# Expert stages with a reordered head and with the branch for over 192 rows at the stage's end

## The chip, the cores and the metric

The kernel runs on one core of a Trainium2 chip. The metric is the device time of one execution in microseconds (us); the time before is 1676.75 us, the median of three runs (1673.84 to 1679.83).

Engines in the profile: PE is TensorE (PEld its weight loads), DVE is VectorE, ACT is ScalarE, POOL is GpSimd, SP is SyncE, which mostly issues DMAs. A name with a q (DVEq) is the engine's queue: register loads, branches, semaphore and DMA-issuing instructions, which don't count as busy.

## The reference

A decoder trunk of two layers over 512 tokens of 1024 features, in fp32. Layer 0 mixes tokens with RWKV-7 and layer 1 with forgetting attention; each is followed by the same kind of expert layer (16 experts, the two best of one group of four for each token), and every sublayer ends in a residual sum and a layer norm:

```python
def shared_router_moe(h, router_w, router_bias, w_gate, w_up, w_down):
    s = jax.nn.sigmoid((xt @ router_w).astype(jnp.float32))
    s_sel = (s + router_bias).reshape(n_tok, N_GROUPS, EXPERTS_PER_GROUP)
    g_star = jnp.argmax(jnp.sum(lax.top_k(s_sel, 2)[0], -1), -1)
    ...
    gate = gate / jnp.sum(gate, -1, keepdims=True)
    ...
    def expert_block(args):
        xb, e = args
        hid = jax.nn.silu(xb @ w_gate[e]) * (xb @ w_up[e])
        return hid @ w_down[e]
    ...
def reference(...):
    for i in range(DEPTH):
        ...
        h = layer_norm(ALPHA * h + mixed, ...)
        ffn = shared_router_moe(h, ...)
        h = layer_norm(ALPHA * h + ffn, ...)
```

The lines left out pick the two best experts (`e_idx`) of the group, and sum each row of `expert_block`'s result, times its gate, into its token; `mixed` is the layer's token mixer, and DEPTH is 2. Each expert has a gate and an up matrix of 1024 x 512 and a down matrix of 512 x 1024. How many tokens an expert gets is known only when the kernel runs.

## The kernel before, in words

The order of stages is RWKV (about 0 to 519 us of the profiled execution), the experts of layer 0 (to 905), attention (to 1250), the experts of layer 1 (to 1640), and the last sum and layer norm. The program is scheduled by hand: on each engine instructions run in the order in which the code issues them.

Products keep fp32 accuracy by splitting each operand into a high part and a remainder (fp32r): ScalarE copies the high part (L199 for weights), VectorE subtracts (L202), and three matmuls add up one product (L68 to L70). Weights come in pieces of 1 MB, six for an expert: a ring of eight raw buffers and six pairs of split buffers. `wsplitA(m)` is the high copy of piece m, `wsplitB(m)` (also called `loA`) the subtraction, which then issues the load of piece m+8 on SP.

An expert stage is `moe` (L178). Its head:

- six high copies on ScalarE (L204), and the routing on VectorE (L207 to L229);
- `rows(n)` finds with one-hot matmuls which tokens the first two experts get, `gather` (L250) fetches 128 rows of the activations `hd` with an indirect DMA on POOL, and `gather2` (L257) the rows 129 to 192 of an expert as pairs of half rows into `xo`;
- `cnt`, the number of rows of each expert, `most`, the largest of them, and the subtraction of piece 0 (L262 to L267);
- `xposeT`/`xposeS` (L274) transpose and split the first expert's rows into Xm; `xposeB` (L303) does it with `xo`, into Xh; then the late loads (pieces 6 and 7, in layer 0 only, issued on ScalarE's queue) and `loA(1)`;
- the tables: VectorE computes for each slot the token, the target row and the gate (L394 to L417); eight scatters on POOL write them to `tab` in DRAM (L426), two loads bring them back as TB and TB2 (L430, L432);
- the If on `most>192` (L435), with `rest` for rows over 192 of an expert inside it. The data of this case never has so many, so every engine jumps over the body, and yet all go through it: they load `most` into a register, branch, and add to their semaphores. The body is 48 copies of `rest`, and it reloads the first six pieces (`again`) and pieces 6 and 7, and transposes the first rows again;
- `count(0)`, `count(1)` load an expert's row count into a register of all five engines; then `loA(2)` to `loA(5)`.

Then the loop over 16 experts: `count(e+2)`, `more(e)` (L338, an If on more than 128 rows: `guB`, `hidBT`, `dnB`, `outB` on the rows 129 to 192), the gathers for later experts, and `expert(e)` (L351): `guA` is gate and up, `dnA` is down, `outA` copies a half of the result, `scatter` (L333) writes the rows to `yd`. Between these an expert splits the next expert's weights and transposes its rows. `outB` (L331) writes its rows into `ys[0]` (`yt` in the profile) for the first expert; `gates0` (L418) makes the first expert's gate by matmul, so that it needs no table.

Behind the stage, `Combine.load_y` (L474) loads `yd` on SP (L478), ScalarE scales the residual (L481), PE adds (L486), and in layer 0 also spreads the norm's weights (L468, L471); VectorE does the layer norm.

Of the kernel before, what the change touches and what calls it, by code (L numbers as in the profile page):

```python
# [13 lines left out]
NR,NH,NM=8,6,6*NE  # L14
# [47 lines left out]
def split(C, hi, lo, src):  # L62
    nc=C.nc
    nc.scalar.activation(hi,src,AF.Copy)  # L64
    nc.vector.tensor_tensor(lo,src,hi.bitcast(F32),op=ALU.subtract)  # L65
# [107 lines left out]
def place(raw, L, W, m, queue):  # L173
    e,j=divmod(m,6); w,hf,kk,n=MAT[j]; M=W[w][L,ORDER[e]]
    queue.dma_start(raw.rearrange("p (k n) -> p k n",k=kk),(M[:,hf*n:(hf+1)*n] if w==1 else M[hf*128*kk:(hf+1)*128*kk,:]).rearrange("(k p) n -> p k n",p=128))


def moe(C, L, W, hd, load, tail, late=()):  # L178
# [4 lines left out]
    with ExitStack() as ctx:  # L183
# [13 lines left out]
        def wsplitA(m,q=None):  # L197
            if m<NM+tail:
                Q=slice(None) if q is None else QS[q]; nc.scalar.activation(his[m%NH][:,Q],raws[m%NR][:,Q],AF.Copy)  # L199
        def wsplitB(m,q=None):  # L200
            if m<NM+tail:
                Q=slice(None) if q is None else QS[q]; V.tensor_tensor(los[m%NH][:,Q],raws[m%NR][:,Q],his[m%NH][:,Q].bitcast(F32),op=ALU.subtract)  # L202
                if q!=0: load(m+NR)
        for m in range(NH): wsplitA(m)  # L204
        loA=wsplitB
        ss=su[:,0:64].rearrange("p (a b) -> p a b",b=4)
# [37 lines left out]
        def rows(n, e, oh, slots):  # L244

            for i in range(NT): V.tensor_scalar(oh[:,i,:],slots,posm[:,i,e:e+1],None,op0=ALU.is_equal)
            for i in range(NT):
                for c in range(2): nc.tensor.matmul(px[:,n:n+1],oh[:,i,:],C.aux[:,i,c:c+1],start=(i+c==0),stop=(i+c==NT))
            V.tensor_scalar(i01[:,n:n+1],px[:,n:n+1],8192.0,None,op0=ALU.add)
        def gather(ix,xg,n):  # L250
            nc.gpsimd.indirect_dma_start(out=xg[0:n],out_offset=None,in_=hd[:,:],  # L251
                in_offset=bass.IndirectOffsetOnAxis(ap=ix[0:n],axis=0),bounds_check=T-1,oob_is_err=False)
        for e in range(2): rows(e,e,oh[e],C.slots); gather(i01[:,e:e+1],xgs[e],128)

        oh2=ys[1][:,256:512].bitcast(BF16).rearrange("p (t n) -> p t n",t=NT); rows(2,0,oh2,C.slots2); i2=p1.tile([128,1],I32,name="i2")
        V.tensor_scalar(i2,i01[:,2:3],2.0,C.odd,op0=ALU.mult,op1=ALU.add)
        def gather2(e):  # L257

            nc.gpsimd.indirect_dma_start(out=xo,out_offset=None,in_=hd.rearrange("t (h n) -> (t h) n",h=2),  # L259
                in_offset=bass.IndirectOffsetOnAxis(ap=TB2[:,4*e+1,3:4] if e else i2,axis=0),bounds_check=2*T-1,oob_is_err=False)  # L260
        gather2(0)
        cnt=p1.tile([1,NE],I32,name="cnt"); V.tensor_copy(cnt,pp[0:1,NT,:])  # L262
        rs={}
        def count(e):
            if e<NE: rs[e]=nc.values_load(cnt[0:1,ORDER[e]:ORDER[e]+1],min_val=0,max_val=T,skip_runtime_bounds_check_because="a count of 512 tokens")
        most=p1.tile([1,1],I32,name="most"); V.tensor_reduce(most,cnt,axis=AX.X,op=ALU.max)
        loA(0); V.tensor_copy(sel,selb)  # L267

# [3 lines left out]
        def slot(m): return his[m%NH],los[m%NH]  # L272
        src=lambda e,b=0: TB[:,4*e+b,0:1]; dst=lambda e,b=0: TB[:,4*e+b,1:2]; gate=lambda e,b=0: TB[:,4*e+b,2:3].bitcast(F32); gate2=lambda e,b=0: TB2[:,4*e+b,2:3].bitcast(F32)
        def xposeT(xg,hf,bk):  # L274
            for k in range(4): nc.tensor.transpose(k4(bk)[:,k,:],xg[:,(hf*4+k)*128:(hf*4+k+1)*128],C.ident)  # L275
        def xposeS(hf,bk): split(C,Xm[:,0,hf*4:hf*4+4,:],Xm[:,1,hf*4:hf*4+4,:],k4(bk))
# [26 lines left out]
        def xposeB():  # L303
            pt=tr[0].rearrange("p (k t h) -> p h k t",k=4,h=2)
            for k in range(4): nc.tensor.transpose(k4(tr[0])[:,k,:],xo[:,k*128:(k+1)*128],C.ident)
            X=Xh.rearrange("p (h k) t c -> p h k t c",h=2)
            for h in range(2): split(C,X[:,h,:,:,0],X[:,h,:,:,1],pt[:,h])
# [43 lines left out]
        def expert(e):  # L351
            f,fo=(gate(e),None) if e else (None,g0[:,0:1]); y=ys[e%2]; w=[slot(6*e+j) for j in range(6)]
            X=xgs[(e+1)%2]; next_=e+1<NE
            hi=lambda j,*q: wsplitA(6*e+6+j,*q); lo=lambda j,*q: wsplitB(6*e+6+j,*q)
            guA(w[0],0); hi(0); lo(0)
            guA(w[1],1); siluA(); hi(1)
            if e==0: gates0(0)
            guA(w[2],2); mulA(0,f); hi(2); lo(1)
            guA(w[3],3,range(6)); hidT(0); hidS(0)
            guA(w[3],3,range(6,8)); mulA(1,f)  # L360
            if next_: xposeT(X,0,tr[1]); xposeS(0,tr[1])
            hi(3,0); lo(2,0)
            dnA(w[4],4,0); hidT(1); hidS(1); hi(3,1); lo(2,1)
            dnA(w[4],4,1)
            if next_: xposeT(X,1,tr[1]); xposeS(1,tr[1])
            hi(4); lo(3)
            dnA(w[5],5,0); outA(0,y,fo)
            if next_: xposeB()
            lo(4); dnA(w[5],5,1); outA(1,y,fo); scatter(dst(e),y,128); hi(5); lo(5)
        def again(e,j):  # L370
            r=raws[6+j%2]; w=slot(6*e+j); place(r,L,W,6*e+j,nc.gpsimd); split(C,*w,r); return w
        def rest(e,blk):

            f=gate(e,blk); ix=dst(e,blk)
            if blk==1: V.memset(i2[0:64],int(BIG)); V.tensor_copy(i2[64:128],ix[64:128]); ix=i2
            gather(src(e,blk),ys[0],128)
            for hf in range(2): xposeT(ys[0],hf,tr[hf]); xposeS(hf,tr[hf])
            for j in range(6):
                w=again(e,j)
                if j<4: guA(w,j)  # L380
                if j==1: siluA()
                if j in (2,3): mulA(j-2,f); hidT(j-2); hidS(j-2)
                if j>3:
                    for n in range(2): dnA(w,j,n)
            for n in range(2): outA(n,ys[0])
            scatter(ix,ys[0],128)

        for hf in range(2): xposeT(xgs[0],hf,tr[hf]); xposeS(hf,tr[hf])
        xposeB()
        for m in late: load(m,nc.scalar)  # L390
        loA(1)

        bl=su[:,256:320].rearrange("p (a b) -> p a b",b=NE); code=su[:,320:384].rearrange("p (a b) -> p a b",b=NE); pos=pp[:,0:NT,:]
        V.tensor_scalar(bl,pos,127.5,None,op0=ALU.is_gt)  # L394
# [36 lines left out]
        t2=tab[0:4096,:]  # L431
        nc.gpsimd.dma_start(TB2,bass.AP(tensor=t2.tensor,offset=t2.offset,ap=[[256,64],[0,2],[1,256]]))  # L432
        nc.gpsimd.tensor_scalar(TB2[:,:,3],TB2[:,:,0],2.0,C.odd,op0=ALU.mult,op1=ALU.add)

        with tc.If(nc.values_load(most[0:1,0:1],min_val=0,max_val=T,skip_runtime_bounds_check_because="a count of 512 tokens")>192):  # L435
            for e in range(NE):
                count(e)
                for blk in (1,2,3):
                    with tc.If(rs[e]>max(192,128*blk)): rest(e,blk)
            for j in range(NH): again(0,j)  # L440
            for m in (6,7): load(m,nc.gpsimd)
            for hf in range(2): xposeT(xgs[0],hf,tr[hf]); xposeS(hf,tr[hf])
        for e in range(2): count(e)
        for m in range(2,NH): loA(m)
        for e in range(NE):
            count(e+2)
            more(e)
            if e+2<NE or e==0: gather(src(2) if e==0 else src(e+2),xgs[e%2],128)
            if e+1<NE: gather2(e+1)
            expert(e)  # L450
    return yd

class Combine:
# [937 lines left out]
```

## Time and profile before

| | |
|---|---|
| median of three runs | 1676.75 us (1673.84 to 1679.83) |
| profiled execution | 1676.42 us, span 1674.7 us |
| granted TensorE clock, mean | 0.923 |
| PE busy | 1486.3 us, 89% of the span |
| VectorE busy | 1172.9 us, 70% |
| ScalarE busy | 926.9 us, 55% |
| POOL busy | 517.1 us, 31% |
| DMA | 317.77 MB, mean 190 GB/s |

Times of instructions count from the start of the span; 1.7 us of the profiled execution lie outside it. [...] A steady expert keeps PE almost fully busy, the stretches between two stages and a stage's head do not.

### The profile page before, as it was taken

What the parts mean: (1) busy time and instruction counts of PE and PEld (TensorE: products, weight loads), DVE (VectorE), ACT (ScalarE), POOL (GpSimd) and SP (SyncE); (2) the same over time, 40 slices, a digit from 0 to 9 for tenths busy, and PEclk for the clock granted to TensorE, in tenths of its full rate; (3) what the DMA queues carried; (4) which work ended last, traced back from release to release, by engine and by line L of the source; (5) the groups of instructions that cost most, each with busy time, mean ns of one, the idle gap of its engine ahead of it and who ended that gap; (6) DMA issues with size and microseconds to landing.
All of it is one profiled execution on the core that took longest, in us unless ns stands there. A gap on an engine that the chain in (4) does not pass through costs nothing. (4 is left out here: it accounts for less than half of the span.)

```text
span 1674.7 us, 25018 instructions
## 1 busy us (share of the span) xinstructions
PE 1486.3 (89%) x9185; PEld 1202.8 (72%) x9185; DVE 1172.9 (70%) x1883; ACT 926.9 (55%) x1361; POOL 517.1 (31%) x423
## 2 busy tenths in 40 slices
PE   6998976989984799999999799999973999999995
PEld 2587765977763688888886677777763788888883
DVE  7547769576785497877996637556545696869984
ACT  2543764534334386867885446555333686858863
POOL 4104776313331333322431422111013232413421
PEclk8998997788986899999999899999985999999998
DMA  7326532033515598897994323112433697979963
GB/s 216 120 82 217 155 97 69 13 121 95 172 68 178 185 340 297 300 350 251 353 353 169 102 82 113 63 36 75 151 107 134 227 370 237 362 243 353 350 235 152
DMA packets 203605, 317.77 MB, mean 190 GB/s; under 512 B 27978, under 2 KB 123554, under 8 KB 203444
## 3 DMA queue, kind: packets, MB, share of 16 engines
q1 hardware_dynamic: 181060, 276.13, 48.4%
q0 software_dynamic: 17664, 33.11, 5.8%
q10 hardware_dynamic: 4720, 6.44, 1.1%
q8 instruction: 93, 1.52, 0.4%
q14 instruction: 68, 0.56, 0.1%
HBM read 304.80 MB, written 37.55 MB: 204 GB/s over the span
## 5 line engine op out<-in xcount | busy, mean ns | idle before, releaser
L202 DVE TENSOR_TENSOR wl<-raw,wh 128x2048 fp32r<-128x2048 f32 (+1 forms) x168 | 334.5, 2005 | 16.9 <-DMA tab<-rec,idx 6.5
L199 ACT ACTIVATE wh<-raw 128x2048 fp32r<-128x2048 f32 (+1 forms) x168 | 282.6, 1688 | 13.3 <-ACT wh L199 8.7
L68 PE MATMUL bank<-wh,xm 128*128 128x256 f32 (+1 forms) x768 | 250.2, 326 | 3.9
L69 PE MATMUL bank<-wl,xm 128*128 128x256 f32 (+1 forms) x768 | 245.4, 320 | 0.0
L70 PE MATMUL bank<-wh,xm 128*128 128x256 f32 (+1 forms) x768 | 245.2, 319 | 0.0
L334 POOL DMA_INDIRECT yd<-yt,TB x38 | 91.5, 2407 | 447.8 <-ACT yt L301 387.5
L68 PEld LDWEIGHTS bank<-wh,xm 128*128 128x128 f32 x768 | 144.7, 188 | 26.1 <-issue 14.6
L69 PEld LDWEIGHTS bank<-wl,xm 128*128 128x128 f32 x768 | 144.8, 189 | 11.4
L70 PEld LDWEIGHTS bank<-wh,xm 128*128 128x128 f32 x768 | 144.7, 188 | 11.3
L202 DVE TENSOR_TENSOR wl<-rawo,wh 128x2048 fp32r<-128x2048 f32 (+1 forms) x56 | 110.2, 1980 | 20.6 <-ACT wh L199 20.1
L68 PE MATMUL bank<-wh,wh 128*128 128x512 f32 x256 | 112.7, 440 | 3.1 <-DVE wl L1082 1.7
L68 PE MATMUL bank<-wh,hm 128*128 128x512 f32 x256 | 111.3, 435 | 2.9 <-ACT hm L64 2.9
L70 PE MATMUL bank<-wh,wl 128*128 128x512 f32 x256 | 102.1, 399 | 2.8 <-DVE wl L1268 2.8
L69 PE MATMUL bank<-wl,wh 128*128 128x512 f32 x256 | 101.5, 397 | 0.0
L70 PE MATMUL bank<-wh,hm 128*128 128x512 f32 x256 | 101.4, 396 | 0.0
L69 PE MATMUL bank<-wl,hm 128*128 128x512 f32 x256 | 100.9, 394 | 0.0
L199 ACT ACTIVATE wh<-rawo 128x2048 fp32r<-128x2048 f32 (+1 forms) x56 | 93.4, 1668 | 12.8 <-PE bank L70 9.0
L1090 POOL TENSOR_TENSOR wl<-raw,wh 128x512 fp32r<-128x512 f32 x29 | 40.8, 1418 | 87.7 <-ACT wh L1089 87.7
L259 POOL DMA_INDIRECT xo<-hd,TB x30 | 61.9, 2063 | 13.0 <-issue 8.0
L65 DVE TENSOR_TENSOR xm<-bank,xm 128x512 fp32r<-128x512 f32 x64 | 44.3, 692 | 29.8 <-ACT xm L64 26.9
L64 ACT ACTIVATE xm<-bank 128x512 fp32r<-128x512 f32 x64 | 38.3, 598 | 47.7 <-PE bank L275 38.8
L68 PEld LDWEIGHTS bank<-wh,wh 128*128 128x128 f32 x256 | 49.6, 194 | 16.4 <-issue 5.6
(545 smaller groups left out, 3557.7 us busy)
## 6 DMA issues: line engine op xcount, KB each, us to landing
raw<-in_moe_w_gate_dram SPq DMA_DIRECT2D x48, 1024.0 KB, 8.4
raw<-in_moe_w_up_dram SPq DMA_DIRECT2D x48, 1024.0 KB, 9.9
raw<-in_moe_w_down_dram SPq DMA_DIRECT2D x48, 1024.0 KB, 7.1
rawo<-in_moe_w_up_dram SPq DMA_DIRECT2D x16, 1024.0 KB, 5.6
rawo<-in_moe_w_down_dram SPq DMA_DIRECT2D x16, 1024.0 KB, 7.8
rawo<-in_moe_w_gate_dram SPq DMA_DIRECT2D x14, 1024.0 KB, 8.9
raw<-in_fx_w_in_dram SPq DMA_DIRECT2D x12, 1024.0 KB, 6.6
raw<-in_rw_wk_dram SPq DMA_DIRECT2D x4, 1024.0 KB, 12.4
```

The lines of the kernel that those rows point to most:

```text
L64: nc.scalar.activation(hi,src,AF.Copy)
L65: nc.vector.tensor_tensor(lo,src,hi.bitcast(F32),op=ALU.subtract)
L68: nc.tensor.matmul(out,ah,bh,start=start,stop=False)
L69: nc.tensor.matmul(out,ah,bl,start=False,stop=False)
L70: nc.tensor.matmul(out,al,bh,start=False,stop=stop)
L199: Q=slice(None) if q is None else QS[q]; nc.scalar.activation(his[m%NH][:,Q],raws[m%NR][:,Q],AF.Copy)
L202: Q=slice(None) if q is None else QS[q]; V.tensor_tensor(los[m%NH][:,Q],raws[m%NR][:,Q],his[m%NH][:,Q].bitcast(F32),op=ALU.subtract)
L259: nc.gpsimd.indirect_dma_start(out=xo,out_offset=None,in_=hd.rearrange("t (h n) -> (t h) n",h=2), in_offset=bass.IndirectOffsetOnAxis(ap=T ...
L334: st=nc.gpsimd.indirect_dma_start(out=yd[:,:],out_offset=bass.IndirectOffsetOnAxis(ap=ix[0:n],axis=0), in_=y[0:n],in_offset=None,bounds_ch ...
L1090: (V if d else G).tensor_tensor(lo[n][:,Q],raw[:,Q],hi[n][:,Q].bitcast(F32),op=ALU.subtract)
```

## The change

The diff, cut to its changed lines:

```diff
@@ -201,6 +201,7 @@
                 if q!=0: load(m+NR)
+        for m in late: load(m,nc.scalar)
         for m in range(NH): wsplitA(m)
@@ -250,7 +251,8 @@
-        for e in range(2): rows(e,e,oh[e],C.slots); gather(i01[:,e:e+1],xgs[e],128)
+        def first(e): rows(e,e,oh[e],C.slots); gather(i01[:,e:e+1],xgs[e],128)
+        first(0)
 
...
@@ -259,10 +261,12 @@
         gather2(0)
+        first(1)
         cnt=p1.tile([1,NE],I32,name="cnt"); V.tensor_copy(cnt,pp[0:1,NT,:])
...
+        for e in range(2): count(e)
         most=p1.tile([1,1],I32,name="most"); V.tensor_reduce(most,cnt,axis=AX.X,op=ALU.max)
         loA(0); V.tensor_copy(sel,selb)
@@ -367,8 +371,6 @@
-        def again(e,j):
-            r=raws[6+j%2]; w=slot(6*e+j); place(r,L,W,6*e+j,nc.gpsimd); split(C,*w,r); return w
         def rest(e,blk):
@@ -376,7 +378,7 @@
             for j in range(6):
-                w=again(e,j)
+                r=raws[6+j%2]; w=his[2+j%4],los[2+j%4]; place(r,L,W,6*e+j,nc.sync); split(C,*w,r)
@@ -385,10 +387,6 @@
-        for hf in range(2): xposeT(xgs[0],hf,tr[hf]); xposeS(hf,tr[hf])
-        xposeB()
-        for m in late: load(m,nc.scalar)
-        loA(1)
 
...
@@ -431,16 +429,8 @@
         nc.gpsimd.tensor_scalar(TB2[:,:,3],TB2[:,:,0],2.0,C.odd,op0=ALU.mult,op1=ALU.add)
-
-        with tc.If(nc.values_load(most[0:1,0:1],min_val=0,max_val=T,skip_runtime_bounds_check_because="a count of 512 tokens")>192):
-            for e in range(NE):
-                count(e)
-                for blk in (1,2,3):
-                    with tc.If(rs[e]>max(192,128*blk)): rest(e,blk)
-            for j in range(NH): again(0,j)
-            for m in (6,7): load(m,nc.gpsimd)
-            for hf in range(2): xposeT(xgs[0],hf,tr[hf]); xposeS(hf,tr[hf])
-        for e in range(2): count(e)
+        for hf in range(2): xposeT(xgs[0],hf,tr[hf]); xposeS(hf,tr[hf])
+        loA(1); xposeB()
         for m in range(2,NH): loA(m)
         for e in range(NE):
             count(e+2)
@@ -448,6 +438,12 @@
             expert(e)
+
+        with tc.If(nc.values_load(most[0:1,0:1],min_val=0,max_val=T,skip_runtime_bounds_check_because="a count of 512 tokens")>192):
+            for e in range(NE):
+                count(e)
+                for blk in (1,2,3):
+                    with tc.If(rs[e]>max(192,128*blk)): rest(e,blk)
     return yd
```

In words: the late loads of layer 0 are issued before the six high copies; the gather of the first expert's half rows comes before that of the second expert's rows; the first two counts are loaded before piece 0 is subtracted; the table arithmetic and its scatters come before the first transposes, and `loA(1)` before `xposeB`. The If with `rest` stands behind the last expert, where the six split pieces of the first expert are no longer needed, so nothing is reloaded or transposed again in it; its weight loads are on SP's queue instead of POOL's.

## Rows read from the trace of the kernel before

**Rows 1.** Busy us (instructions) by stretch: stretch, length, engines, granted clock, DMA share, GB/s

```profile
520.00:552.00 32.00, 6.86 (x52) 4.96 (x53) 18.38 (x74) 13.67 (x11) 11.35 (x12) 0.50 0.69 240
...
593.00:612.00 19.00, 18.85 (x113) 16.28 (x113) 17.14 (x16) 15.46 (x16) 6.81 (x3) 1.00 0.98 332
```

**Rows 2.** Timeline, layer 0's head: start, us, engine, line, operation, out<-in, xcount [idle <-releaser]

```profile
528.88 2.29 DVE L202 TENSOR_TENSOR wl<-raw,wh 128x2048 fp32r<-128x2048 f32 x1
...
533.29 1.49 DVE L65 TENSOR_TENSOR xm<-bank,xm 128x512 fp32r<-128x512 f32 x2 [2.02 <-ACT xm L64]
...
537.22 1.09 PE L305 MATMUL bank<-ident,xo 128*128 128x128 f32 x4 [3.80 <-DMA xo<-hd,i]
...
539.23 0.95 ACTq L175 DMA_DIRECT2D rawo<-in_moe_w_gate_dram  x2
539.65 0.43 DVE L65 TENSOR_TENSOR xh<-bank,xh 128x256 fp32r<-128x256 f32 x1 [0.46 <-ACT xh L64]
540.00 2.28 DVE L202 TENSOR_TENSOR wl<-raw,wh 128x2048 fp32r<-128x2048 f32 x1
542.19 0.22 DVE L394 TENSOR_SCALAR su<-bank 128x64 f32<-128x64 f32 x1
...
547.15 0.40 DVE L416 CAST gp<-gr 128x4 bf16<-128x4 f32 x1
```

**Rows 3.** Timeline, layer 0, where the pair phase and the next subtractions begin

```profile
551.60 0.80 PE L309 MATMUL bank<-wl,xh 128*128 128x512 f32 x1 [3.74 <-DVEq L435]
...
554.02 8.90 DVE L202 TENSOR_TENSOR wl<-raw,wh 128x2048 fp32r<-128x2048 f32 x4 [6.47 <-DMA tab<-rec,idx]
```

**Rows 4.** Line L435, both layers: ns min/median/max, first and last start us, forms

```profile
L435 PEldq COMPARE_BRANCH  x2: 3718/3842/3967, 538.6 to 1275.2; - x2
...
L435 ACTq COMPARE_BRANCH  x2: 45/45/45, 541.3 to 1276.9; - x2
...
L435 POOLq TENSOR_LOAD <-most x2: 321/416/512, 571.2 to 1306.7; - x2
...
L435 POOLq INC_SWDGE_SEM  x2: 583/873/1163, 574.9 to 1310.2; - x2
```

**Rows 5.** Line L265 on ScalarE's queue, the heads of layers 0 and 1

```profile
L265 ACTq TENSOR_LOAD <-cnt x3: 278/280/291, 547.1 to 547.8; - x3
...
L265 ACTq TENSOR_LOAD <-cnt x3: 277/279/323, 1279.7 to 1280.4; - x3
```

**Rows 6.** Timeline, layer 0: expert 0's first matmul, the sum of outB, expert 1's first

```profile
569.48 0.40 PE L68 MATMUL bank<-wh,xm 128*128 128x512 f32 x1
...
576.17 0.68 DVE L331 TENSOR_TENSOR yt<-xo,bank 64x512 f32<-64x512 f32 x1 [9.68 <-DMA TB<-tab]
...
592.52 0.47 PE L68 MATMUL bank<-wh,xm 128*128 128x512 f32 x1
```

**Rows 7.** Timeline, layer 1: first transposes, pair phase, first matmuls of experts 0 and 1

```profile
1271.46 1.94 PE L275 MATMUL bank<-ident,xg 128*128 128x128 f32 x8 [9.91 <-DMA xg<-hd,i]
...
1288.07 0.79 PE L309 MATMUL bank<-wl,xh 128*128 128x512 f32 x1 [6.54 <-DVEq L435]
...
1304.63 0.39 PE L68 MATMUL bank<-wh,xm 128*128 128x512 f32 x1
...
1327.26 0.47 PE L68 MATMUL bank<-wh,xm 128*128 128x512 f32 x1
```

**Rows 8.** Timeline at the two stage ends: last scatter, loads of yd, scaling, adds

```profile
905.63 1.00 POOL L334 DMA_INDIRECT yd<-yt,TB  x1 [14.03 <-ACT yt L301]
...
908.33 0.34 SPq L478 DMA_DIRECT2D rawo<-yd  x1
...
1639.97 3.88 ACT L481 ACTIVATE raw<-raw 128x1024 f32<-128x1024 f32 x4
...
1641.07 7.13 PE L486 MATMUL bank<-raw,ident 128*128 128x512 f32 x16 [1.63 <-ACT raw L481]
...
1643.06 0.33 SPq L478 DMA_DIRECT2D rawo<-yd  x1
```

## The prediction

> **What bounds the kernel now.** I read the page's busy line first, then the busy shares by stretch, then the timeline around the branch at L435, then what that line's instructions do on each engine. The shares by stretch show two regimes [rows 1]. In a steady expert PE has work for 18.85 of 19.00 us: TensorE is the bound there, and nothing that the other engines save changes the time. In the head of a stage PE is busy for 6.86 of 32.00 us at half the clock: there the serial order of routing, gathers, tables and the first transposes sets the end, and each microsecond taken out of that chain moves all sixteen experts forward. So the change is priced in four places: two heads and two stage ends.
>
> In the head of layer 0 VectorE does the first expert's subtraction, then stands still for the gather, does xposeS, stands still again until the gather of the odd half rows lands (PE's transposes at L305 had waited 3.80 us for it), does the two halves of xposeB, then loA(1), and only then the table arithmetic [rows 2]. Then it walks through the If at L435. PE's phase of 64-row pairs (L309, guB in more(0)) starts one matmul, then waits for DVEq L435, that is for VectorE's passage through a branch whose body is not executed; the second matmul is at 551.60, and loA(2) to loA(5) begin at 554.02 behind it [rows 3]. The reader should see there that the releaser is a queue instruction, not data.
>
> The passage itself is dear [rows 4]: PE's compare-and-branch takes 3.7 to 4.0 us; ScalarE's takes 45 ns, but the engine's next instruction, the first count load, comes 5.8 us after it in layer 0 (541.3 to 547.1) and 2.8 us in layer 1 (1276.9 to 1279.7) [rows 4, 5]; POOL needs 3.7 and 3.5 us from its load of `most` to its INC_SWDGE_SEM, and that takes up to 1.2 more. POOL comes to this If last, behind the tables' landing, and holds the next thing up: VectorE's sum into yt (L331) waits 9.68 us, until 576.17, and expert 0 takes 23.04 us from its first guA matmul to that of expert 1, against 19.00 [rows 1, 6].
>
> **The change, part by part.**
>
> Head of layer 0. Removed from the path: the If, and the standstill before xposeB, because the table arithmetic now fills it. New order on VectorE: the counts, loA(0), sel, tables, xposeS, loA(1), xposeB. Before, loA(0) ran from 528.88 to 531.17 and sel closely behind it. The two counts come ahead of it now: a register load from SBUF takes 0.3 to 0.5 us on POOL and the three on ScalarE start over 0.7 us [rows 4, 5]; two of them with the wait on cnt I take as 1.0 (0.6 to 1.6). With 0.1 for sel, VectorE is free at 532.3, and the tables, 542.19 to 547.55 or 5.36 us, end at 537.65. xposeS 1.49 brings 539.15, loA(1) 2.28 brings 541.45, two xposeB subtractions of 0.43 with ScalarE's second copy between them (0.46) bring 542.8 [rows 2]. PE's phase then runs from about 542.9 instead of 551.60 less the half matmul that it had done early, 551.2 [rows 3]. Gain 8.3. loA(2) to (5) start then too, at the distance from guB that they have now.
>
> What is late next would be the gather. The two late loads, 2.1 MB, now share the DMA engines with the gathers instead of coming after them; at the stretch's mean of 240 GB/s [rows 1] that is 8.7 us of traffic. If all of it stood in front of the gather of xo, which lands at 537.2 now, the transposes would start at 545.9 and guB 2.9 us later (537.22 to 540.08, the end of xposeB, now), at 548.8: gain 2.4. If it costs nothing and the counts are at their lower end, 9.0. I take 8.3, because xposeS of the first gather now comes 4 us later than before, and xo is now second instead of third on POOL's queue. The two issues of the late loads (0.95 for both [rows 2]) go in front of ScalarE's six hi copies and delay each by as much; loA(0), which reads the first, starts a microsecond later too, so this is hidden. The gather of expert 1 moves behind xo; its rows are needed in the middle of expert 0. Tables, scatters and TB loads start 10 us earlier on POOL and DVE; nothing waits for them any longer in expert 0. The counts on PE, ScalarE, POOL and SP lie in front of the waits for the gather, hidden by those; SP has load(8) behind them, which waits for loA(0) anyway.
>
> Expert 0 of layer 0. With no If on POOL ahead, the sum into yt waits only for ScalarE's copy; ScalarE's hi(0) then follows and the weight splits run as in a steady expert. 19.0 and a margin of 0.4, which I chose, for its twelve small gate matmuls is 19.4 against 23.04: gain 3.6 (0 to 4.0).
>
> Layer 1 has no late loads. Its first gather is itself late: PE's transposes start at 1271.46 after 9.91 us of waiting for it [rows 7]. The tables (5.36) and the counts (1.0) fit into that wait. 1.94 for the transposes, with ScalarE's copy under them, 1.49, 2.28 and 1.32 (0.43, 0.46, 0.43) [rows 2] bring guB to 1278.5, against 1288.07, less half a matmul, 1287.7: gain 9.1 (7 if the counts delay a gather's issue by two, 12 if POOL's issue comes three earlier). Expert 0: 1327.26 less 1304.63 is 22.63, less 19.4: gain 3.2 (0 to 3.6).
>
> The four gains sum to 24.2; low ends 9.4, high ends 28.6. Later experts pass them on, since PE bounds these.
>
> Stage ends. The If now stands between expert 15 and what follows. End of layer 0: the last scatter is issued at 905.63 and takes 1.00; SP's first load of yd follows at 908.33, when it has landed [rows 8]. Behind the scatter POOL now loads `most`, branches, is silent and runs INC_SWDGE_SEM: 3.5 to 3.7 and 0.6 to 1.2, so 4.1 to 4.9 [rows 4], to 910.7 or 911.5. Everything that reads yd waits on that, as yt did in the head: 2.4 to 3.2, I take 2.8. ScalarE's passage, 0.4 and 2.8 [rows 4, 5], runs beside it; where it takes 5.8 the end costs 6.2. PE's 4.0 and its load, 4.4, lie beside ScalarE's passage, behind which the copies and the scaled rows come; only what exceeds that shows.
> End of layer 1: the same 2.8 for SP's load at 1643.06. ScalarE's scaling (1639.97) comes 3.2 later, PE's adds with it, at 1644.3, after an idle stretch of 4.8 instead of 1.63. The sixteen take 7.13 us now [rows 8]; in the heads' idle stretches the granted clock is 0.50 [rows 1], and all sixteen at that would cost 7.1 more. I take about a microsecond of it: 4.0 (2.4 to 10). Both ends: 6.8. [...]
>
> [...]
>
> Sum: the profiled execution took 1676.42 us (span 1674.7), 0.33 below the median of 1676.75. 1676.42 - 24.2 + 6.8 = 1659.0.
>
> **The rivals.**
> A, the forecast: 1659, own range 1653 to 1664.
> B, expert 0 keeps its length (the sum into yt is freed, but splits or scatters wait on another thing). For: the row of yt names the landing of TB<-tab as its releaser [rows 6]. Against: that sum reads no table, its wait ends with POOL's passage, and the tables land some 10 us earlier too. 24.2 less 6.8 is 17.4, so net 17.4 - 6.8 = 10.6: 1666.
> C, dear ends: ScalarE's long silence at the first and PE at the low clock at the second, 6.2 and 10. 24.2 - 16.2 = 8: 1668. For: 5.8 was measured once of two; against: that one fell beside 240 GB/s of loads.
> D, cheap ends or earlier gathers: gain 27, ends 2: 1651. For: POOL's and PE's sequencers may run ahead of their engines; against: in the heads nothing shortened the passage. [...]
> E, slower: the far jump is paid in series at each end. PE passes only when its last products are done, 4.4; ScalarE passes after it, 6.2; POOL's 4.9 follows: 15.5 an end, 31 in all, against 24.2: 1683. It decides from 12.1 an end. Against: in rows 4 and 5 the engines pass independently, each when its own queue arrives.
> F, the gather becomes the bound in layer 0 and expert 0 keeps its length in both: low ends, 9.4 - 6.8 = 2.6: 1673.8, no change by the measure below.
>
> **How the numbers follow.** A 0.50, B 0.12, C 0.14, D 0.12, E 0.06, F 0.06. A measurement of this kernel tells no change from 0.3%, 5.0 us. A to D are faster, 0.88, of which I move 0.01 to no change for a C that is worse; F gives 0.06 and with that 0.07; E 0.06. The range from 1649 to 1671 holds A to D with the ends' bounds and leaves out F and E, 0.12, with a little of D's tail.
>
> **What would show it.** Right: the L309 matmuls of the pair phase run without a gap and no DVEq of the big If stands before them; yt's sum at L331 has no long idle; expert 0 takes about 19.4; the If's branch appears after the last scatter, and SP's load of yd comes 5.5 us behind the scatter's issue, not 2.7. Wrong: PE's transposes of xo or xg after 540 in layer 0 (F); expert 0 still at 22 to 23 (B); ScalarE silent for more than 5 us at an end, or PE's clock at 0.5 during the adds of the last stage (C); yd loads within 1 us of today's distance (D); PE's first work after expert 15 later than ScalarE's (E).

## The result

The changed kernel takes 1648.49 us, the median of four runs (1646.16 to 1651.01), against 1675.3 before, also the median of four (1673.08 to 1679.83): a ratio of 0.9841, with a 95% interval from 0.9819 to 0.9862. The forecast was 1659.0 with a range from 1649 to 1671; the result lies just below the range. The direction was right, the gain 27 us instead of 17.

The profiled execution of the changed kernel has a span of 1649.3 us, 25.4 below that of before. The span falls into pieces that are the same in every kernel of this study: the routing sigmoid of each layer on ScalarE (519.20 and 1252.72 before), the first matmul of expert 0 at L68, the last scatter of the layer (905.63 and 1640.35 before), the end. Differences of these times, us:

| piece | before | after | change | forecast |
|---|---|---|---|---|
| start to sigmoid, layer 0 (RWKV) | 519.20 | 516.86 | -2.34 | 0 |
| sigmoid to expert 0, layer 0 | 50.28 | 38.43 | -11.85 | -8.3 |
| expert 0 to last scatter | 336.15 | 332.38 | -3.77 | -3.6 |
| last scatter to sigmoid, layer 1 | 347.09 | 351.06 | +3.97 | +2.8 |
| sigmoid to expert 0, layer 1 | 51.91 | 38.14 | -13.77 | -9.1 |
| expert 0 to last scatter | 335.72 | 332.36 | -3.36 | -3.2 |
| last scatter to end | 34.35 | 40.04 | +5.69 | +4.0 |

The first piece is no effect: RWKV is untouched, and over the sixteen kernels traced here it took between 511.4 and 524.4 us. Without it the change is worth 23.1 us in the traces, or 1.4%, the least gain that the interval of the ratio allows; no piece of the traces shows the rest of the medians' 26.8. RWKV also is why times of one kernel lie several us apart, and why small effects below are read from the pieces.

The head of layer 0 in the timeline after, to be held against [rows 2, 3, 6]:

```profile
516.86 0.22 ACT L1312 ACTIVATE s<-rb 128x64 f32<-128x64 f32 x1 [1.27 <-PE rb L159]
...
527.83 2.29 DVE L202 TENSOR_TENSOR wl<-raw,wh 128x2048 fp32r<-128x2048 f32 x1
...
530.14 0.21 DVE L392 TENSOR_SCALAR su<-bank 128x64 f32<-128x64 f32 x1
...
535.17 1.28 DVE L65 TENSOR_TENSOR xm<-bank,xm 128x512 fp32r<-128x512 f32 x2
535.80 1.00 POOL L424 DMA_INDIRECT tab<-rec,idx  x1 [0.30 <-issue]
535.91 1.12 PE L309 MATMUL bank<-ident,xo 128*128 128x128 f32 x4 [2.11 <-DVE xm L65]
536.37 2.28 DVE L202 TENSOR_TENSOR wl<-raw,wh 128x2048 fp32r<-128x2048 f32 x1
...
539.64 0.63 PE L313 MATMUL bank<-wl,xh 128*128 128x512 f32 x1
539.79 8.95 DVE L202 TENSOR_TENSOR wl<-raw,wh 128x2048 fp32r<-128x2048 f32 x4
...
548.65 0.15 DVE L421 COPY g<-bank 128x1 f32<-128x1 f32 x1
548.91 0.87 DVE L321 TENSOR_SCALAR su<-bank,g 128x256 f32<-128x256 f32 x2
...
551.46 0.50 PE L313 MATMUL bank<-wh,hs 128*128 128x512 f32 x1 [0.46 <-DVE hs L65]
...
555.24 0.68 DVE L335 TENSOR_TENSOR yt<-xo,bank 64x512 f32<-64x512 f32 x1 [2.94 <-ACT xo L335]
555.29 0.40 PE L68 MATMUL bank<-wh,xm 128*128 128x512 f32 x1
...
574.65 0.47 PE L68 MATMUL bank<-wh,xm 128*128 128x512 f32 x1
```

The tables start right behind loA(0), no queue instruction of the If releases the pair phase (now L313), and the sum into yt waits 2.94 us for ScalarE instead of 9.68. Expert 0 takes 574.65 - 555.29 = 19.36 us. The last four subtractions end at 548.74; expert 0 begins 6.55 us later. In [rows 3, 6] that distance is the same: 554.02 + 8.90 to 569.48 is 6.56. So VectorE's sixth subtraction dates the start of expert 0 in both kernels: only behind it does VectorE copy the gate (L421) and scale the pair phase's up products (L321), from which the rows `hs` of that phase's last sixteen matmuls are made. In layer 0 after the change PE is as late: `hs` starts 2.21 us behind the end of the phase's weight products on PE, and no head of any run has less than 2.19.

The If, now at L442, engine by engine; the columns are those of [rows 4]:

```profile
L442 PEldq COMPARE_BRANCH  x2: 3475/3576/3677, 884.0 to 1605.5; - x2
L442 ACTq TENSOR_LOAD <-most x2: 285/286/287, 886.8 to 1608.4; - x2
...
L442 POOLq TENSOR_LOAD <-most x2: 298/300/302, 887.4 to 1609.0; - x2
...
L442 POOLq INC_SWDGE_SEM  x2: 1530/1812/2093, 891.2 to 1612.4; - x2
```

PE's branch begins at 884.0, ahead of layer 0's last scatter (887.67), while its products still run (to 886.76); POOL's begins at 887.8, while that scatter runs (1.00 us). What PE's next matmuls wait for is ScalarE's passage. They spread the norm's weights (L464, L468 before); first before, then after:

```profile
904.65 3.69 PE L468 MATMUL bank<-raw,raw 1*128 1x512 f32 x8
```

```profile
890.00 5.57 PE L464 MATMUL bank<-raw,raw 1*128 1x512 f32 x8 [3.25 <-ACTq L442]
```

Their granted clock, of which 1.0 is TensorE's full speed, is 1.00 before and 0.65 after. SP's first load of yd comes 5.83 us behind this scatter (893.50) instead of 2.7.

And the end of layer 1 after, against [rows 8]:

```profile
1609.23 1.00 POOL L338 DMA_INDIRECT yd<-yt,TB  x1 [14.05 <-ACT yt L305]
1611.40 3.90 ACT L477 ACTIVATE raw<-raw 128x1024 f32<-128x1024 f32 x4 [2.45 <-ACTq L442]
1612.52 10.20 PE L482 MATMUL bank<-raw,ident 128*128 128x512 f32 x16 [4.20 <-ACT raw L477]
1614.22 0.34 SPq L474 DMA_DIRECT2D rawo<-yd  x1
```

SP's load comes 4.99 us behind the scatter instead of 2.7, PE's adds wait 4.20 and then take 10.20 us instead of 7.13. The third column from the right is the granted clock during them, before and after:

```profile
1641.07:1648.20 7.13, 7.13 (x17) 3.31 (x18) 0.00 (x0) 4.06 (x4) 0.28 (x1) 1.00 0.58 203
```

```profile
1612.52:1622.72 10.20, 10.20 (x17) 4.43 (x18) 0.00 (x0) 4.06 (x4) 0.00 (x0) 0.70 0.75 273
```

### The profile page after: what moved, and what is told of

It reads as the page before. It is cut to its first block, busy times and chain, and to the rows that moved or that the text cites. A ratio compares the mean times of both kernels' runs of the same rounds, so it can differ in the third digit from the quotient of the medians.

```text
span 1649.3 us, 25004 instructions
## 1 busy us (share of the span) xinstructions
PE 1485.4 (90%) x9185; PEld 1199.9 (73%) x9185; DVE 1173.0 (71%) x1883; ACT 924.3 (56%) x1359; POOL 519.3 (31%) x423
## 5 line engine op out<-in xcount | busy, mean ns | idle before, releaser
L202 DVE TENSOR_TENSOR wl<-raw,wh 128x2048 fp32r<-128x2048 f32 (+1 forms) x168 | 334.5, 2005 | 5.6 <-DVEq L345 5.6
L68 PE MATMUL bank<-wh,xm 128*128 128x256 f32 (+1 forms) x768 | 249.8, 325 | 3.9
L68 PEld LDWEIGHTS bank<-wh,xm 128*128 128x128 f32 x768 | 144.6, 188 | 26.1 <-issue 14.6
L202 DVE TENSOR_TENSOR wl<-rawo,wh 128x2048 fp32r<-128x2048 f32 (+1 forms) x56 | 110.2, 1980 | 24.9 <-ACT wh L199 24.4
L68 PE MATMUL bank<-wh,wh 128*128 128x512 f32 x256 | 112.4, 439 | 3.1 <-DVE wl L1078 1.7
L68 PE MATMUL bank<-wh,hm 128*128 128x512 f32 x256 | 111.3, 435 | 0.0
L64 ACT ACTIVATE xm<-bank 128x512 fp32r<-128x512 f32 x64 | 38.3, 598 | 46.4 <-PE bank L279 45.3
L68 PEld LDWEIGHTS bank<-wh,wh 128*128 128x128 f32 x256 | 49.4, 193 | 16.4 <-issue 5.7
L1221 ACT ACTIVATE sb<-sb,st 128x512 f32<-128x512 f32 (+1 forms) x64 | 35.7, 559 | 45.7 <-DVE st L1217 29.3
```

What stands on the lines that cost most here:

```text
L68: nc.tensor.matmul(out,ah,bh,start=start,stop=False)
L1221: S.activation(SB[u][:,0:N],SB[u][:,0:N],AF.Exp,bias=ST[u][:,0:1],scale=-1.0,accum_out=ST[u][:,1:2])
```

## The experiments

Each ratio is to the kernel before, timed beside the variant; the changed kernel was not timed beside them, so variants are held against it by the pieces of their traces. The pieces of each run's profile (us; columns as in the table above, the last one is the whole from the first sigmoid to the end):

| kernel | RWKV | head 0 | experts 0 | to layer 1 | head 1 | experts 1 | end | from sigmoid |
|---|---|---|---|---|---|---|---|---|
| before | 519.2 | 50.3 | 336.1 | 347.1 | 51.9 | 335.7 | 34.3 | 1155.5 |
| after | 516.9 | 38.4 | 332.4 | 351.1 | 38.1 | 332.4 | 40.0 | 1132.4 |
| If moved alone | 513.4 | 45.0 | 333.5 | 350.8 | 48.0 | 333.5 | 39.9 | 1150.7 |
| If in the head | 520.3 | 46.4 | 332.5 | 347.6 | 46.4 | 332.5 | 34.3 | 1139.7 |
| no If | 514.2 | 38.8 | 332.4 | 347.8 | 38.2 | 332.3 | 34.3 | 1123.8 |
| short body | 518.0 | 38.5 | 332.4 | 347.6 | 38.2 | 332.4 | 34.9 | 1123.9 |
| counts late | 517.7 | 39.8 | 332.3 | 350.9 | 43.7 | 332.4 | 38.7 | 1137.8 |
| counts early only | 522.0 | 48.9 | 333.7 | 346.2 | 50.6 | 336.6 | 34.4 | 1150.4 |
| load 8 in the code later | 514.0 | 52.6 | 334.7 | 347.9 | 51.8 | 335.2 | 34.4 | 1156.6 |
| load 8 behind | 520.9 | 51.4 | 332.2 | 346.5 | 49.5 | 335.2 | 34.3 | 1149.2 |
| tables first | 516.9 | 41.9 | 332.5 | 352.4 | 41.7 | 332.5 | 38.9 | 1139.9 |
| piece 1 on POOL | 517.7 | 42.4 | 332.3 | 351.9 | 42.9 | 332.2 | 39.7 | 1141.5 |
| piece 1 left out | 514.3 | 37.8 | 332.4 | 351.6 | 37.6 | 332.3 | 38.6 | 1130.5 |
| warm end, 24 | 524.4 | 39.1 | 332.3 | 351.9 | 38.1 | 332.3 | 39.7 | 1133.6 |
| warm end, 11 | 511.4 | 38.8 | 332.4 | 351.6 | 39.7 | 332.4 | 37.1 | 1132.0 |
| POOL and warm end, 24 | 516.5 | 41.9 | 332.5 | 350.9 | 42.9 | 332.5 | 39.2 | 1140.0 |

**The If moved alone.** The kernel before, with

```diff
-        with tc.If(...most...>192):
-            ...
         for e in range(2): count(e)
         for m in range(2,NH): loA(m)
         for e in range(NE):
...
             expert(e)
+        with tc.If(...most...>192):
+            ...
```

> The kernel before with one part alone: the If on most>192 stands at the stage's end (its body with SP loads into the freed slots), the head keeps its old order. Theory T (VectorE's passage through the If held PE's pair phase, POOL's passage held the sum into yt): no queue instruction of that If stands before the second L309 matmul any more; the pair phase starts near 540 in layer 0 but is now held by loA(2), which still waits for the tables; expert 0 shrinks from 23.0 and 22.6 to about 19.4 us in both layers. Heads 8.5 and 6.7, expert 0 3.6 and 3.3, ends -4.0 and -5.7 as in the changed kernel: 12 us faster than before, about 1663. In layer 1 the first transposes stay some 18.7 us behind the routing sigmoid. Rival R1 (the new order brings the gain, and the If costs the same wherever it stands): within 3 us of the kernel before, expert 0 unchanged or its gain lost at the end.

Measured: 1669.43 us against 1673.43, ratio 0.9985 (0.9964 to 1.0007). The theory's price was too high, though its mechanism shows: the second matmul of the pair phase comes 21.0 us behind the sigmoid in layer 0 instead of 32.4, and expert 0 loses 2.6 and 2.2 us of its stall. But the head gains 5.3 and 3.9, not 8.5 and 6.7, since loA(2) stands behind the tables and the ends take back 9. In sum the pieces give 4.8 us of the 12 forecast, and by time alone this kernel can't be told from the one before; most of the change's gain is not in the If's place alone.

**The new order alone**, the If back in the head between the tables and the first transposes:

```diff
+        with tc.If(...most...>192):
+            ...
+            for j in range(NH): again(0,j)
+            for m in (6,7): load(m,nc.gpsimd)
         for hf in range(2): xposeT(xgs[0],hf,tr[hf]); xposeS(hf,tr[hf])
         loA(1); xposeB()
```

> The changed kernel with its new order, but the If (with the reloads it needs there) in the head, between the tables and the first transposes. Theory T: VectorE's passage (3 to 4 us) again lies before the first subtraction of xposeS, POOL's again before the sum into yt: expert 0 back to 22.5 to 23 us, heads 3.7 longer each, ends 4.0 and 5.7 shorter: about 5 us slower than the changed kernel, 1653, still 22 faster than before. Rival R1 (order alone): the pair phase starts as in the changed kernel, 22.3 us behind the sigmoid, expert 0 stays near 19.4, and the ends' 9.7 come on top as a gain: about 1640.

Measured: 1656.95, ratio 0.99 (0.9871 to 0.9929). Each head is 8 us longer than the changed kernel's, the ends are back at 34.3, together 7.3 slower than the changed kernel. The forecast's passage of 3.7 was too small, as PE's first transposes now wait for it too: the pair phase starts 6.5 and 7.4 us later. In layer 0 another 1.5 us come from a lower clock in that phase's last sixteen matmuls (5.4 instead of 3.8 us, see the clock below), not from the If. Expert 0 stayed short, against the theory:

```profile
541.95 1.97 PE L279 MATMUL bank<-ident,xg 128*128 128x128 f32 x8 [12.57 <-DVEq L435]
...
566.67 0.39 PE L68 MATMUL bank<-wh,xm 128*128 128x512 f32 x1
...
569.46 0.68 DVE L335 TENSOR_TENSOR yt<-xo,bank 64x512 f32<-64x512 f32 x1 [7.31 <-DMA TB<-tab]
...
570.99 1.92 ACT L199 ACTIVATE wh<-rawo 128x2048 fp32r<-128x2048 f32 x1
```

The sum into yt still waits for POOL's passage, but the earlier tables bring that forward: the sum comes 2.8 us behind expert 0's first matmul instead of 6.7 [rows 6], and ScalarE's first high copy 4.3 us behind it, exactly as in the changed kernel. That it is POOL's passage which holds the sum, and not the landing of the table that the bracket names, shows in all eight heads of these runs in which it waits so long: it starts 0.06 to 0.09 us behind the end of POOL's INC_SWDGE_SEM. The pieces: the If moved gives 4.8, the order 15.8, both 23.1.

**What the stage ends cost.** Without the If at all, and with a body of one copy (both leave out rows over 192 of an expert, of which this data has none):

```diff
-            for e in range(NE):
-                count(e)
-                for blk in (1,2,3):
-                    with tc.If(rs[e]>max(192,128*blk)): rest(e,blk)
+            rest(0,1)
```

> The changed kernel without the If and its body (rows over 192 of an expert are left out; the data has none). Theory T: the stage ends cost what the passage adds: SP's first load of yd comes 2.6 us behind the last scatter instead of 5.6 and 4.7, the sixteen adds at the end take about 7 us instead of 10.2, and 9 to 10 us are saved: about 1639. Rival R2 (the ends are longer for another reason, the clock or the loads of the next stage shifted in time): less than 4 us saved.

> The changed kernel with the If's body cut to one copy of rest instead of 48 (other rows over 192 are left out; the data has none). All waits and semaphores of the If stay, only the jump is short. Theory T (the silence behind the branch is the fetch of a far target): PE's compare-and-branch falls from 3.5 to under 0.5 us, ScalarE's, VectorE's and POOL's silences of 2.8 to 3.4 us to under 0.5; POOL's INC_SWDGE_SEM of 1.5 to 2.1 stays; 4 to 7 us faster than the changed kernel, about 1643. Rival R3 (the passage is waiting for the engine's own work and semaphores): silences and time as in the changed kernel within 2 us.

Measured: 1640.39, ratio 0.9814 (0.9786 to 0.9843), and 1639.25, ratio 0.9802 (0.9773 to 0.9831). Without the If the two ends are 3.3 and 5.7 shorter; with the short body they are 3.5 and 5.1 shorter, although every wait and semaphore stands. L442 with the short body:

```profile
L442 PEldq COMPARE_BRANCH  x2: 313/322/330, 885.2 to 1603.3; - x2
...
L442 ACTq COMPARE_BRANCH  x2: 45/45/45, 888.4 to 1606.5; - x2
L442 ACTq EVENT_SEMAPHORE  x2: 17/17/17, 888.7 to 1606.7; - x2
L442 POOLq TENSOR_LOAD <-most x2: 300/300/301, 888.7 to 1606.8; - x2
...
L442 POOLq INC_SWDGE_SEM  x2: 1527/1801/2075, 889.3 to 1607.4; - x2
```

PE's branch falls from 3.6 to 0.32 us, ScalarE goes on 0.3 us behind its branch (888.4 to 888.7) instead of 2.8 (887.1 to 889.9), VectorE 0.2 instead of 3.1, SP 0.2 instead of 4.6 (these three in layer 0), and POOL's way from the register load to INC_SWDGE_SEM from 3.8 and 3.4 to 0.6, while INC_SWDGE_SEM itself stays at 1.5 to 2.1: shown is that the price hangs on the length of what is jumped over. The profile also counts the DMA packets that bring instructions. In 12 us around the end of layer 0 (883 to 895, and 884 to 896) they are nine in the changed kernel and one with the short body:

```profile
q14 instruction: 7, 0.06, 1.6%
q8 instruction: 2, 0.03, 1.3%
```

```profile
q8 instruction: 1, 0.02, 0.5%
```

The silences and these packets go together, as theory T has it; how long an engine waits for one such packet, no run here shows.

**The first gather of layer 1.** In the kernel before, PE's first transposes came 18.7 us behind the sigmoid, after the change 14.6, at the same time of POOL's issue (10.2). Before, the gather fell into VectorE's subtraction:

```profile
1262.18 2.28 DVE L202 TENSOR_TENSOR wl<-raw,wh 128x2048 fp32r<-128x2048 f32 x1
1262.96 2.46 POOL L251 DMA_INDIRECT xg<-hd,i  x1 [6.97 <-DVE most L266]
```

After, the early counts let the gather start first, and the next gather is the one that is held:

```profile
1248.95 1.07 POOL L252 DMA_INDIRECT xg<-hd,i  x1 [6.96 <-DVE cnt L265]
1249.40 2.29 DVE L202 TENSOR_TENSOR wl<-raw,wh 128x2048 fp32r<-128x2048 f32 x1
1250.33 2.26 POOL L261 DMA_INDIRECT xo<-hd,i  x1 [0.30 <-issue]
```

The counts were put back in the changed kernel, and brought forward alone in the kernel before:

```diff
-        for e in range(2): count(e)
         most=p1.tile([1,1],I32,name="most"); ...
...
         loA(1); xposeB()
+        for e in range(2): count(e)
```

> The changed kernel with the two early counts put back behind xposeB, so that VectorE starts loA(0) 1.2 us earlier. Theory H (an indirect gather that POOL begins while VectorE's subtraction L202 runs is held until it ends, and its data then meets load(8)): in layer 1 the first gather, issued 10.2 us behind the sigmoid, falls into L202 again and takes 2.3 to 2.5 us instead of 1.07; PE's first transposes come 18.7 us behind the sigmoid instead of 14.6, the pair phase at 24.4 instead of 22.0. In layer 0 its first two gathers are issued before L202, so there only the 1.2 us show: pair phase at 21.0 instead of 22.2. Together about 1 us slower than the changed kernel. Rival D (load(8) competes for the DMA engines, no hold): the gather's instruction stays at 1.07, first transposes at 16 to 17. Rival O (the tables' place made the gather early, not the counts): transposes stay at 14.6 and the kernel is 2 us faster.

> The kernel before with one part alone: the two counts ahead of loA(0). Theory H: in layer 1 L202 starts behind the first gather's issue, the gather takes 1.07 instead of 2.46 us and lands earlier: first transposes 14.6 us behind the sigmoid instead of 18.7. The If still holds the pair phase, so of that some 3 us reach it (second L309 at 32 instead of 35.35), while layer 0 loses about 1: net 2 us faster. Rival O: transposes stay at 18.7.

Measured: 1656.88 for the first, ratio 0.9884 (0.9842 to 0.9926); 1674.18 for one run of the second. With the counts late:

```profile
1240.73 0.22 ACT L1312 ACTIVATE s<-bank 128x64 f32<-128x64 f32 x1 [1.27 <-PE bank L159]
...
1250.18 2.29 DVE L202 TENSOR_TENSOR wl<-raw,wh 128x2048 fp32r<-128x2048 f32 x1
1250.97 2.45 POOL L252 DMA_INDIRECT xg<-hd,i  x1 [6.98 <-DVE most L269]
```

The transposes come 18.9 us behind the sigmoid, and 14.9 in the other kernel, whose gather takes 1.08: both as theory H said. But the head of layer 1 grew by 5.5, more than the 2.9 by which the pair phase starts later, and that of layer 0 by 1.4 instead of shrinking. The counts now delay loA(2) (VectorE is no earlier at its sixth subtraction in layer 0), and the phase's last sixteen matmuls take 5.4 instead of 3.8 us. The clock column of the stretches shows why, first with the counts late, then the changed kernel:

```profile
552.20:557.60 5.40, 5.40 (x17) 4.31 (x18) 0.54 (x3) 0.91 (x2) 1.51 (x3) 0.68 0.80 289
```

```profile
551.50:555.30 3.80, 3.80 (x17) 3.08 (x18) 0.49 (x3) 0.90 (x2) 0.68 (x2) 1.00 1.05 399
```

In the kernel before, the early counts alone gain 1.3 in the head of layer 1, since the If still holds PE. The head of layer 0, for which a loss of 1 was forecast, gains 1.4: there the gather of `xo` had been the held one, and it takes 1.00 us instead of 2.43.

Then the load that competes with the gather. In a first try its line was moved behind xposeB:

```diff
-                if q!=0: load(m+NR)
+                if q!=0 and m!=0: load(m+NR)
...
-        loA(1)
+        load(NR); loA(1)
```

> The kernel before with one load moved: piece 8 is loaded behind xposeB instead of behind loA(0); loA(0) stays where it is. It tells the hold from the competing load. Theory H: in layer 1 the first gather's instruction still takes about 2.4 us and ends 0.9 behind L202, but its data meets no 1 MB load: first transposes near 16 us behind the sigmoid (18.7 before). Rival D (load alone): instruction 1.07, transposes near 14.6. Rival: neither matters, 18.7.

It moved nothing: SP has no other work there and issued the load at 1261.00, right behind the subtraction's end at 1260.97; the transposes stayed at 18.7. So it went to ScalarE's queue, which gets there only after the transposes (`load(NR,nc.scalar)`):

> The kernel before with piece 8 loaded on ScalarE's queue behind xposeB, so that it is issued only after the first transposes (on SP, in the run before, it was issued at the old time). Theory H (hold and load together): in layer 1 the first gather's instruction still takes 2.45 us, held by L202, and the transposes come at about 16 us behind the sigmoid, because the 1 MB is gone from the gathers' time. Rival D (load alone): instruction 1.07, transposes 14.6. Rival G (the hold alone, the load costs nothing): 18.7 as before.

The transposes came 16.2 us behind the sigmoid, with the gather's instruction still at 2.45 us: of the 4.1 us, 2.5 are the load's traffic, and the other 1.6 go with the hold (the gather's instruction alone is 1.4 us longer than 1.07), as H expected.

**Tables ahead of loA(0).**

```diff
-        for e in range(2): count(e)
...
-        loA(0); V.tensor_copy(sel,selb)
+        V.tensor_copy(sel,selb)
...
-        loA(1); xposeB()
+        loA(0); xposeB()
+        for e in range(2): count(e)
+        loA(1)
```

> The changed kernel with VectorE's head reordered once more: tables directly behind the routing, then xposeS, loA(0), xposeB, the two counts, loA(1). Theory: VectorE is the bound of the new head, and the tables fill its wait for the gather, which no subtraction holds: first transposes at 14.6 us behind the sigmoid in layer 1 and about 15 in layer 0, pair phase at 20.3 instead of 22.2 and 22.0, stage ends unchanged: about 4 us faster than the changed kernel, 1644.5. Rival: the first two split pieces, now later, hold PE in the pair phase, or the first gather lands no earlier: within 1 us of the changed kernel.

Measured: 1660.12, ratio 0.9905 (0.9869 to 0.9942), heads of 41.9 and 41.7. The pair phase began 1.4 and 1.3 us earlier, but the sixth subtraction ended 2 us later (34.0 and 33.6 us behind the sigmoid instead of 31.9 and 31.6), because VectorE waited for the gather with the subtractions still ahead of it. Expert 0 followed the sixth subtraction, not the pair phase; the other 1.3 and 1.5 us of the longer heads are the lower clock in the last sixteen matmuls (5.1 and 5.4 us instead of 3.8).

**One subtraction off VectorE.** First onto POOL, as shown; then left out, with `load(1+NR)` in place of `loA(1)` and the remainder `los[1]` set to zero by POOL at the stage's start:

```diff
+        nc.gpsimd.tensor_tensor(los[1],raws[1],his[1].bitcast(F32),op=ALU.subtract); load(1+NR)
...
-        loA(1); xposeB()
+        xposeB()
```

> The changed kernel with one of VectorE's six subtractions of the head (piece 1) on POOL, between its gathers and the table scatters. Theory V (VectorE's work, back to back from the sigmoid to the end of the sixth subtraction, sets the start of expert 0, 6.56 us behind that end): the pair phase starts 1 to 1.3 us earlier (xposeB waits for its transposes part of the 2.28), the sixth subtraction ends 1.3 to 2.3 earlier, expert 0 starts 1.3 to 2.2 earlier in each layer: 2.5 to 4.5 us in all. Rival: POOL's subtraction takes 6 us or more beside VectorE's and slows it, or the tables come late: no gain or a loss.

Measured: 1659.55, ratio 0.9898 (0.9867 to 0.9929): both heads over 4 us longer. POOL's subtraction and VectorE hold each other up:

```profile
528.64 2.29 DVE L202 TENSOR_TENSOR wl<-raw,wh 128x2048 fp32r<-128x2048 f32 x1
529.13 6.19 POOL L270 TENSOR_TENSOR wl<-raw,wh 128x2048 fp32r<-128x2048 f32 x1
530.85 4.51 DVE L272 CAST sel<-selb 128x64 f32<-128x64 bf16 x1
```

The copy into sel, 0.18 us otherwise, lasts until POOL is done, at 535.3. In layer 1 a small two-input operation of VectorE (L401, 0.22 us in layer 0) lasts 5.25.

> The changed kernel with VectorE's subtraction of piece 1 left out (its remainder is set to zero on POOL early in the head, so the products with it are missing). It takes 2.28 us off VectorE without new work beside it. Theory V (VectorE, busy without a break from the sigmoid to its sixth subtraction, sets the head): the sixth subtraction ends 1.3 to 2.3 us earlier, the pair phase starts 1.0 to 1.4 earlier (its transposes then take part of it), expert 0 starts 1 to 2.3 us earlier in both layers. Rival P (PE's own pair phase at the low clock is the bound from its start on): expert 0 follows the start of the pair phase alone, at 15.6 us as now; a longer distance would mean the clock fell.

One run, 1646.55 us. The sixth subtraction ends 1.1 and 0.5 us earlier, the pair phase starts 1.1 and 0.4 earlier, expert 0 0.6 and 0.5. So not VectorE's work alone is the bound, but its chain with PE's transposes of xo, which come as late as before; part of the 2.28 us was beside that wait. In layer 1 expert 0 still follows the sixth subtraction at 6.55 us. In layer 0 it follows PE's own weight products of the pair phase, which now end last and take 10.1 us instead of 9.6. Both theories were half right.

**The end of layer 1.** 24 small matmuls (then 11) behind the If:

```diff
+        if L==1:
+            for _ in range(24): nc.tensor.matmul(pgo[:,0:128],C.ident,C.ident,start=True,stop=True)
```

> The changed kernel with 24 small matmuls of constants into an unused bank behind the If of layer 1 (their result is never read): they fill PE's wait for ScalarE there. Theory: the sixteen adds of the last sum took 10.2 instead of 7.1 us because PE's clock fell in the 4.2 us of idle; kept busy it stays at 1.0, the adds take 7.1 and the end is 2.5 to 3 us shorter. Rival: the loads of yd, 2.2 us later too, bound the adds: under 1 us saved.

> As the run with 24 small matmuls of constants behind the last If, but with 11: those 24 ran as 48 passes and delayed the adds themselves by 2.5 us. Theory C (the last stage's end is bound by PE's adds at a low clock): PE is busy until ScalarE's first scaled rows, the adds start with them at full clock, and from the last scatter to the end it takes 37 to 38 us instead of 40.0. Rival L (SP's loads of yd, 2.2 us later than before, bind the adds): 39.5 to 40.

Measured: 1653.32, ratio 0.9846 (0.9809 to 0.9883), and 1648.37, ratio 0.9857 (0.9823 to 0.9891). The 24 ran as 48 passes until 1624.55 and kept the adds waiting; with 11:

```profile
1606.63 2.69 PE L448 MATMUL bank<-ident 128*128 128x128 f32 x22 [1.29 <-PEq L442]
1608.60 3.90 ACT L479 ACTIVATE raw<-raw 128x1024 f32<-128x1024 f32 x4 [2.63 <-ACTq L442]
1609.71 7.13 PE L484 MATMUL bank<-raw,ident 128*128 128x512 f32 x16 [0.39 <-ACT raw L479]
```

The adds take 7.13 us again, and the end 37.1 instead of 40.0: the clock cost 2.9 of the 5.7. SP's first load of yd still comes 5.2 us behind the scatter, so rival L, by which the loads bind the adds, does not hold. By time alone this version can't be told from the changed kernel.

**Piece 1 on POOL with the 24 matmuls**, built on the expectation that both help, which neither does:

> e11 and e12 together: 5 to 7 us faster than the changed kernel, about 1642, if both theories hold; their gains lie in different stages and should add.

Measured: 1657.46, ratio 0.9892 (0.9867 to 0.9917); slower than the changed kernel, as its first part is.

## Why the prediction was wrong

The failed step is the sentence "loA(2) to (5) start then too, at the distance from guB that they have now", and with it the choice of PE's pair phase as the clock of the head. Expert 0 starts 6.56 us behind VectorE's sixth subtraction, in the kernel before too. There loA(2) began 2.4 us behind the pair phase's second matmul [rows 3] (1.1 in layer 1); in the changed kernel it begins 0.15 and 0.1 behind. That is 2.3 of the 3.6 us missed in the head of layer 0. Behind the If, VectorE still had two counts to load into registers, which takes 0.7 us. In layer 1 they are most of the distance: with the counts early and the If in place it is 0.3. In layer 0 it then still is 2.35, so there it comes with the If: VectorE's queue stands still for 1.4 us behind the second count, and for 2.1 without the counts; on what, stays open. The other 1.3: the pair phase begins with the first half of xposeB, which I had counted whole, and xposeS overlaps the end of the tables. (The upper bound of 9.0 for this head should have been 8.7, the 8.3 and 0.4 for the counts at their lower end; nothing hung on it.)

In layer 1, 4.7 us were missed. 1.0 is the same distance; 3.7 is the gather. I had taken its late landing [rows 7] as a thing that stays, bounded by "12 if POOL's issue comes three earlier". The issue did not move at all; the counts, which I had booked as a cost of 1.0 on VectorE, moved the subtraction out of the gather's way and delayed load(8) by as much. Rival D had "earlier gathers" in it and a price of 1651, but for another reason.

Expert 0 (3.6 and 3.2 forecast, 3.8 and 3.4 found) was right in size. Its reason was one of two: the If moved alone gives 2.6 and 2.2 of it, and with the If left in the head the earlier tables give all of it, because POOL then passes the If in time.

The ends were under-priced by 2.9. The passage was near the forecast: SP's first load of yd comes 3.1 and 2.3 us later, where I had 2.8. The clock was not: the last stage's adds lost 3.1 us to the low clock, for which I had put one, and at the first end the spread of the norm's weights lost 1.9 (5.57 instead of 3.69), for which I had put nothing; how much of that 1.9 reaches the end of the stage, no run shows. Rival D's 2 us for both ends were an estimate that no run shows: they cost 9.7 with this body, and 1.1 with a body of one copy. Of the signs, one did not come: the If's branch on PE stands ahead of the last scatter, not behind it.

Against the forecast, the heads gave 8.2 us more and expert 0 0.3 more, the ends cost 2.9 more, and RWKV was 2.3 shorter, which is chance. Without RWKV's share the pieces make 1653, inside the range; that the median fell 0.5 us below it, and not above, is decided by such chance, while the heads were mis-sized in any case.

The clock in the pair phase's last sixteen matmuls stays open. They take 3.8 us at full clock in 24 of the 32 heads, and 5.1 to 5.4 at a mean granted clock of 0.68 to 0.72 in eight: both with the counts late, both with the tables first, layer 0 with the If in the head, with the counts early only and with load 8 later in the code, but also layer 1 of the warm end with 11, whose head is the changed kernel's own. The time since PE's last weight product does not tell them apart: it is 2.9 us in two of the eight, and 4.0 in one of the 24. Where a head's start moves, 1.6 us either way can come with it.

## What to carry to other kernels

Find the last engine of a head by a distance that stays: an instruction whose end stands at the same distance ahead of the next stage in both layers, and in a kernel where it moved, dates it, whatever the waits say in between; look as well which engine is a close second. The If that was never taken cost by the length of its body, on each of the five engines that walked through it: PE's branch took 3.6 us over 48 copies and 0.32 over one. Another place for it gave 4.8 us by itself, and a short body took back 8.6 of the 9.7 us that it cost there, so make the body short first. An instruction that looks like pure cost on one engine can be a gain by what it lets go first; ask of each queue what its next start will run beside.

## What the runs showed of the hardware that was not expected

In these traces a POOL gather that started while one of VectorE's subtractions at L202 ran was held until that ended: it took 2.2 to 2.5 us instead of 1.0 to 1.1 and ended some 0.9 behind it (with the counts late 1250.18 + 2.29 = 1252.47, 1250.97 + 2.45 = 1253.42). One that started 0.4 to 0.6 us ahead of the subtraction delayed neither: in layer 1 of the changed kernel the gather (1248.95, 1.07 us) and the subtraction (1249.40, 2.29 us) overlap at their usual lengths. POOL's own subtraction took 4.5 us in layer 1 and 6.2 in layer 0, where VectorE's ran beside it for the first 1.8, and it kept a copy of VectorE for 4.5. Why the one waits for the other, no run shows.

A stage that no edit touched (RWKV) varied by 13 us between the traces of the sixteen kernels, 511.4 to 524.4, more than most effects tried here.
